# A two-layer attention trunk: PSUM evictions read in steps and written in runs, and the second attention's softmax denominators turned once for four units and applied after the products

## The chip, the cores and the metric

The kernel runs on one core of one Trainium2 chip. The metric is the device time of one execution, in microseconds (us). Before the change three runs gave 1384.46, 1385.28 and 1386.71 us, a median of 1385.28. The profile is one further execution of the same program, which took 1385.48 us; its recorded span is 1383.7 us, and the other 1.8 us lie around it.

Names of engines: PE multiplies matrices (PEld is its weight load), ACT is the scalar engine, DVE the vector engine, POOL the GpSimd engine, and SP issues most DMAs. SBUF is the on-chip memory, PSUM the small memory into which PE writes its products; ACT and DVE evict them from there.

## The reference, cut to what matters

Two layers on a sequence of 1024 tokens of width 1024, everything in float32. Layer 0 is a dilated window attention with 18 heads in three groups of six, layer 1 a latent attention with 16 heads over all 1024 keys.

```python
def dilated_window_attention(q, k, v, bias_table, window, dil):
    ...
    def to_sub(t):
        return t.reshape(B, L, dil, H, Dh).transpose(0, 2, 3, 1, 4)
    ...
def mixer_mla(u, w_in, q_norm, w_uq, kv_norm, w_ukv, w_out):
    ...
        s = (jnp.einsum('bqhd,bkhd->bhqk', qn, k_nope)
             + jnp.einsum('bqhd,bkd->bhqk', qr, k_rope)).astype(jnp.float32) * scale
        p = jax.nn.softmax(s, axis=-1).astype(v.dtype)
        return jnp.einsum('bhqk,bkhd->bqhd', p, v)
    ...
    y = o * jax.nn.silu(gate)
    return y @ w_out
def reference(...):
    for i in range(DEPTH):
        ...
        u = x * (1 + scale) + shift
        ...
        x = layernorm(DEEPNORM_ALPHA * x + gate * y, ln_g[i], ln_b[i])
```

The dilation (4 in the second group, 16 in the third) means that a query meets only the keys of its own class, position modulo the dilation. In layer 1 the softmax divides each query's products by the sum of its 1024 exponentials; the result is multiplied by the gate.

## The kernel before, in words

Every large product is done as three products of float32r halves: a value is split into a high part (ACT casts it) and a low part (DVE or POOL subtracts), and `mm3` (lines 89 to 91) multiplies high by high, high by low and low by high into one PSUM bank.

The order on PE and SP is the order of the program text. ACT, DVE and POOL are ordered at build time by a scheduler that simulates the engines; what it chose is fixed in the built program, and each engine then works strictly in that order. On SP a DMA that waits holds up all DMAs behind it.

**First attention (about 73 to 480 us).** Pairs of heads p = 0 to 8, three pairs to a group. While PE attends for pair p, it also projects q, k and v of pair p+1: each projection is a 128x512 half (`hf`) in a PSUM bank named `pj`, evicted by `a_evac`. For the second group (g = 1, dilation 4) and the third (g = 2, 8 classes) the eviction sorts tokens by class: `a_view` gives the place in SBUF, `src` the order in which the bank is read. Before the change the bank is read in runs and SBUF is written in steps: neighbours in the bank land 256 elements apart (g = 1) or 128 (g = 2). The q of g = 1 goes through ACT twice (line 381, `qh`, one head each, 64x512) and DVE twice (line 383, `ql`), the k likewise (lines 390 and 392), v through ACT once (line 368), and in g = 2 q through ACT (line 371) and k through DVE (line 373). POOL copies `qh` once more (line 386). The same DVE also splits the transposed probabilities of the running attention (line 541, `pt0l`), which PE needs for the products of lines 564 and 572.

Between the two attentions, `merge_lines` combines the three groups' softmax weights. Its line 703 is run three times on 48x128: for g = 0 it reads one operand in a run, for g = 1 and 2 in steps of 32 and 16 elements; it always writes a run.

**Second attention (about 800 to 1290 us).** 128 units u (head u // 8, block u % 8 of 128 queries). `front(u)` is the six score products into a bank pair `s`; `soft(u)` takes the row maximum (DVE, line 1274, `mb`); `expo(u)` takes the exponential of 128x1024 on ACT (line 1280) and leaves the row sums in a column of `mb`; `middle(u-2)` transposes the probabilities (8 PE transposes, line 1293), ACT casts them (line 1296, `pth`) and DVE subtracts (line 1297, `ptl`); `back(w)`, once for two units, does 16 products with v (line 1316) into a bank `o` (named `po` in the code). In `middle` DVE also takes the reciprocal of one unit's row sums (line 1298) and POOL spreads it over 64 columns of `den` (line 1299). `back` transposes `den` on PE (line 1308) ahead of its products, so that the reciprocals lie along the queries; ACT copies both halves of `o` out (lines 1321, 1322, `osum`), DVE multiplies the reciprocals from PSUM with the gate `gT` (line 1325, twice per `back`), and POOL adds the halves and multiplies (lines 1328, 1329). The banks of `t`, `o` and of the projections for coming heads (`m`, made by `b_turn` and `b_qk` in between) come from one ring of four.

`b_weights(p)` fetches the weights of head pair p from DRAM (`wuraw`, `wvraw`, one buffer each) and splits them (ACT; POOL, line 1134, `wul`).

**Tail (about 1290 to 1384 us).** `b_out_blocks(i)` is the output projection of token block i into `po` (two bank pairs in turn, so block i+2 needs block i evicted); its inputs are `ytb`, the split of `gT` (lines 1386, 1387), and the split weights `wo`. `finish(i)` evicts `po` times the gate row (DVE, line 1425, `zb`), adds `x1(i)` (POOL, lines 1419 and 1420, from rows `lnrow` and the DMA `xn_d`), and normalises. SP issues four `lnrow` DMAs (line 801), the gate `row` (line 796) and the `x` blocks (line 1418).

Of the kernel before, what the change touches and what calls it, by code (L numbers as in the profile page):

```python
# [66 lines left out]
class Trunk:  # L67
# [900 lines left out]
    def layer_b_in(self):  # L968
# [3 lines left out]
        nb = self.M.tile([P, 384], F32, name="normb")  # L972
        nc.sync.dma_start(nb, A["bnorm"].to_broadcast([P, 384]))
        nc.vector.tensor_scalar(nb[:, 0:256], nb[:, 0:256], 96.0**-0.5, None, op0=ALU.mult)
        ktab = self.M.tile([P, 8, 2, 16], F32, name="ktab")
# [148 lines left out]

    def b_weights(self, p):

        nc, A, BS = self.nc, self.A, self.BS
        raw = BS.tile([P, 640], F32, tag="wuraw", bufs=1, name=self.nm("wuraw"))
        h = BS.tile([P, 640], F32R, tag="wuh", bufs=1, name=self.nm("wuh"))
        l = BS.tile([P, 640], F32R, tag="wul", bufs=1, name=self.nm("wul"))  # L1130
        n = 384 if p % 2 else 640
        nc.sync.dma_start(raw[:, 0:n], A["wu_o" if p % 2 else "wu_e"][p // 2])
# [3 lines left out]
        if p % 2 == 0:  # L1136
            raw = BS.tile([P, 256], F32, tag="wvraw", bufs=1, name=self.nm("wvraw"))
            h = BS.tile([P, 256], F32R, tag="wvh", bufs=1, name=self.nm("wvh"))
            l = BS.tile([P, 256], F32R, tag="wvl", bufs=1, name=self.nm("wvl"))
            nc.sync.dma_start(raw, A["wv"][p // 2])  # L1140
            nc.scalar.activation(h, raw, AF.Copy)
            nc.gpsimd.tensor_tensor(l, raw, f32(h), op=ALU.subtract)
            self.wv[p // 2] = (h, l)

# [110 lines left out]
    def layer_b_attention(self):  # L1255
        nc = self.nc
        st = {}
# [19 lines left out]
        def expo(u):  # L1277
            s, m = st[u]
            pr = self.ht(F32, "pr")
            nc.scalar.activation(pr, s, AF.Exp, bias=m[:, 0:1], accum_out=m[:, 1:2])  # L1280
            st[u] = (pr, m)

        def middle(u):
            pr, m = st.pop(u)
            a = u % 2
            if a == 0:
                st["pt"] = [(self.gt(F32R, "pth"), self.gt(F32R, "ptl")) for _ in range(2)]
                st["den"] = self.M.tile([P, P], F32, tag="den", bufs=3, name=self.nm("den"))
# [9 lines left out]
            nc.vector.reciprocal(m[:, 2:3], m[:, 1:2])  # L1298
            nc.gpsimd.tensor_copy(st["den"][:, 64 * a : 64 * a + 64], m[:, 2:3].to_broadcast([P, 64]))  # L1299
            if a:  # L1300
                st[("pv", u // 2)] = (st.pop("pt"), st.pop("den"))

        def back(w):
            pts, den = st.pop(("pv", w))
# [3 lines left out]
            nc.tensor.transpose(po[:, 256:384], den, self.ident)  # L1308
            hq = hd % 4
            n = 0  # L1310
            for j in range(2):
                for c in range(4):
                    kt = 4 * j + c
                    v = self.vq[kt // 2][:, (kt % 2) * 512 + hq * P : (kt % 2) * 512 + hq * P + P]
                    for x in range(2):
                        nc.tensor.matmul(po[:, 0:256], v, pts[j][x][:, c * 256 : c * 256 + 256], start=n == 0, stop=n == 15)  # L1316
# [4 lines left out]
            nc.scalar.copy(w3[mine, 0:256], po[other, 0:256])  # L1321
            nc.scalar.copy(w3[mine, 512:768], po[mine, 0:256])
            for a in range(2):
                qs = slice(a * P, a * P + P)
                nc.vector.tensor_tensor(
                    w3[mine, 256 + a * P : 384 + a * P], po[64 * a : 64 * a + 64, 256:384], g[:, qs], op=ALU.mult
                )
            nc.gpsimd.tensor_tensor(w3[mine, 0:256], w3[mine, 512:768], w3[mine, 0:256], op=ALU.add)
            nc.gpsimd.tensor_tensor(g, w3[mine, 0:256], w3[mine, 256:512], op=ALU.mult)
# [4 lines left out]
        for u in range(nu + 4):  # L1334
# [70 lines left out]
    def layer_b_out(self):  # L1405
# [59 lines left out]
        for i in range(7):  # L1465
# [4 lines left out]
            x1(i + 1)  # L1470
            for _ in active:
# [86 lines left out]
```

## Time and profile before

| what | us |
|---|---|
| median of three runs | 1385.28 |
| the profiled execution, total | 1385.48 |
| its span | 1383.7 |
| PE busy | 1340.7 |
| DVE busy | 916.6 |
| ACT busy | 813.4 |
| POOL busy | 578.2 |

How to read the lines below. A row of the waits view says who waited for whom: microseconds in total, how many times, the longest. A row of the timeline is start, duration, engine, line, operation, tiles, shapes, count, and in brackets the idle time before it and what ended it. Matmuls overlap in PE's pipeline, so a matmul's duration is longer than the step from its start to the next start; the steps between starts are what PE's time is made of. A row of the windows view gives for one stretch its length, the busy time of PE, PEld, DVE, ACT and POOL with instruction counts, PE's granted clock (1.00 is full), the DMA share and GB/s. A row of one source line gives its durations in ns (shortest/median/longest), first and last start, and the shapes.

### The profile page before, as it was taken

To read this page: it belongs to the slowest core of one execution; us is meant where nothing else is said; L and a number is where in the kernel's file an instruction comes from. 1 tells how busy PE (TensorE), PEld (TensorE's weight loads), DVE (VectorE), ACT (ScalarE), POOL (GpSimd) and SP (SyncE) were. 2 spreads that over 40 slices of the span, in tenths; PEclk is the share of its full clock that TensorE was granted. 3 is DMA by queue.
4 is the path that set the end of the run, shared out by engine and by line. 5 is a ranking of instruction groups with operands and counts; after the bars stand their busy time and mean duration, and the time that the engine had idled before them with its cause. 6 is when DMAs were issued, how large, how long until landed. Compare 5 with 4: busy or idle time off the path is not lost.

```text
span 1383.7 us, 20921 instructions
## 1 busy us (share of the span) xinstructions
PE 1340.7 (97%) x7439; PEld 1148.6 (83%) x7439; DVE 916.6 (66%) x1688; ACT 813.4 (59%) x1599; POOL 578.2 (42%) x666
## 2 busy tenths in 40 slices
PE   6999999999999999999999999999999999999896
PEld 5788888788888788888988888888889888898785
DVE  6654355455455434666744279888988889888787
ACT  3575566565443432345742288788687878888321
POOL 4442333133122266714732344634553463444653
PEclk9999999999999999999999999999999999999999
DMA  9423221122244255553154011010011000014132
GB/s 354 118 59 49 48 61 40 27 58 77 96 150 125 87 138 141 198 170 118 57 151 145 4 29 22 16 30 17 22 30 31 22 16 17 16 62 145 39 113 86
DMA packets 42168, 110.05 MB, mean 80 GB/s; under 512 B 6277, under 2 KB 12565, under 8 KB 42064
## 3 DMA queue, kind: packets, MB, share of 16 engines
q1 hardware_dynamic: 37512, 96.43, 22.7%
q0 software_dynamic: 4096, 12.24, 3.6%
q8 instruction: 59, 0.97, 0.3%
q14 instruction: 45, 0.37, 0.1%
q10 hardware_dynamic: 456, 0.05, 0.0%
HBM read 92.22 MB, written 8.61 MB: 73 GB/s over the span
## 4 chain that ended last, share of the span: by engine, by line
PE 70%; DVE 15%; ACT 6%; issue 5%; DMA 3%; SPq 0%; DVEq 0%; ACTq 0%
PE pj L89 7%; PE pj L91 7%; PE pj L90 7%; PE o L1316 5%; PE t L1293 5%; DVE mb L1274 3%; PE s L91 3%; PE s L89 3%; PE s L90 3%; PE po L91 3%; PE po L89 3%; PE po L90 3%; PE pg L89 2%; PE pg L91 2%; PE pg L90 2%
## 5 line engine op out<-in xcount | busy, mean ns | idle before, releaser
L89 PE MATMUL pj<-uh,wh 128*128 128x512 f32 x528 | 217.7, 412 | 0.0
L91 PE MATMUL pj<-uh,wl 128*128 128x512 f32 x528 | 207.6, 393 | 0.0
L90 PE MATMUL pj<-ul,wh 128*128 128x512 f32 x528 | 207.3, 393 | 0.0
L1297 DVE TENSOR_TENSOR ptl<-t,pth 128x512 fp32r<-128x512 f32 x256 | 165.3, 681 | 3.0 <-ACT pth L1296 0.9
L1274 DVE TENSOR_REDUCE mb<-s 128x1 f32<-128x1024 f32 x128 | 155.7, 1217 | 7.9 <-PE s L91 6.3
L1280 ACT ACTIVATE pr<-s,mb 128x1024 f32<-128x1024 f32 x128 | 143.4, 1120 | 29.4 <-DVE mb L1274 17.9
L1296 ACT CAST pth<-t 128x512 fp32r<-128x512 f32 x256 | 138.9, 589 | 36.2 <-PE t L1293 34.0
L102 POOL TENSOR_TENSOR wl<-wraw,wh 128x1024 fp32r<-128x1024 f32 x43 | 108.8, 2536 | 91.1 <-ACT wh L101 58.4
L1293 PEld LDWEIGHTS t<-ident,pr 128*128 128x128 f32 x1024 | 119.3, 140 | 19.7 <-DVE ptl L1297 2.6
L1293 PE MATMUL t<-ident,pr 128*128 128x128 f32 x1024 | 133.2, 273 | 1.9 <-DVE ptl L1297 1.9
L1316 PE MATMUL o<-pth,vq 128*128 128x256 f32 x512 | 130.4, 293 | 0.0
L1316 PE MATMUL o<-ptl,vq 128*128 128x256 f32 x512 | 125.5, 283 | 0.8 <-DVE ptl L1297 0.8
L514 ACT ACTIVATE sb<-sb,stat 128x256 f32<-128x256 f32 (+1 forms) x144 | 67.0, 466 | 100.2 <-DVE stat L508 100.1
L91 PEld LDWEIGHTS pj<-uh,wl 128*128 128x128 f32 x528 | 99.4, 188 | 22.3
L1299 POOL COPY den<-mb 128x64 f32<-128x64 f32 x128 | 30.0, 236 | 203.5 <-DVE mb L1298 193.9
L90 PEld LDWEIGHTS pj<-ul,wh 128*128 128x128 f32 x528 | 100.2, 190 | 14.1
L89 PEld LDWEIGHTS pj<-uh,wh 128*128 128x128 f32 x528 | 100.0, 189 | 14.0
L89 PE MATMUL s<-kb,q 128*128 128x512 f32 x256 | 104.5, 408 | 0.4 <-ACT pr L1280 0.4
L91 PE MATMUL s<-kb,q 128*128 128x512 f32 x256 | 101.3, 396 | 0.0
L90 PE MATMUL s<-kb,q 128*128 128x512 f32 x256 | 100.9, 394 | 0.0
L1316 PEld LDWEIGHTS o<-ptl,vq 128*128 128x128 f32 x512 | 97.8, 191 | 1.4 <-DVE ptl L1297 1.4
L1316 PEld LDWEIGHTS o<-pth,vq 128*128 128x128 f32 x512 | 97.7, 191 | 0.2
(286 smaller groups left out, 3252.7 us busy)
## 6 DMA issues: line engine op xcount, KB each, us to landing
wraw<-wa SPq DMA_DIRECT2D x36, 512.0 KB
ada<-ada_row SPq DMA_DIRECT2D x64, 256.0 KB
wraw<-wo_a SPq DMA_DIRECT2D x18, 512.0 KB
ada<-ada_ss SPq DMA_DIRECT2D x16, 512.0 KB
kb<-kb POOLq DMA_DIRECT2D x30, 256.0 KB, 3.0
f<-f_d SPq DMA_DIRECT2D x18, 256.0 KB
xc<-xt SPq DMA_DIRECT2D x8, 512.0 KB
xr<-x SPq DMA_DIRECT2D x8, 512.0 KB
```

The source lines that it names most:

```text
L89: mm(out, wh, xh, start=start, stop=False)
L90: mm(out, wh, xl, start=False, stop=False)
L91: mm(out, wl, xh, start=False, stop=stop)
L102: (lo_engine or self.nc.gpsimd).tensor_tensor(l[:, :width], raw[:, :width], f32(h[:, :width]), op=ALU.subtract)
L514: nc.scalar.activation(sb[:, a * w : a * w + w], sb[:, a * w : a * w + w], AF.Exp, bias=stat[:, 0, hh, t : t + 1], scale=-1.0, accum_out=s ...
L1274: nc.vector.tensor_reduce(m[:, 0:1], s, axis=AX.X, op=ALU.max, negate=True)
L1280: nc.scalar.activation(pr, s, AF.Exp, bias=m[:, 0:1], accum_out=m[:, 1:2])
L1293: nc.tensor.transpose(pt[:, c * P : c * P + P], pr[:, kt * P : kt * P + P], self.ident)
L1296: nc.scalar.copy(h, src)
L1297: nc.vector.tensor_tensor(l, src, f32(h), op=ALU.subtract)
L1299: nc.gpsimd.tensor_copy(st["den"][:, 64 * a : 64 * a + 64], m[:, 2:3].to_broadcast([P, 64]))
L1316: nc.tensor.matmul(po[:, 0:256], v, pts[j][x][:, c * 256 : c * 256 + 256], start=n == 0, stop=n == 15)
```

## The change

Two things are changed together, with some moves beside them.

1. In `a_view` and `a_evac` the loops over class and position are exchanged. The same elements go to the same places; now the bank is read in steps (4 or 8 elements of 4 bytes) and SBUF is written in runs of 128 or 64.
2. In the second attention the exponentials' row sums go to a tile `den` of eight columns for a head. After every fourth unit DVE takes one reciprocal of four columns. `back` no longer transposes for each pair; every second `back` transposes four columns (4x128) behind its products. `spread` copies these four rows to SBUF (ACT), writes them to DRAM and reads them back into 64 partitions (two DMAs on SP, `den_d` and `rden`). POOL multiplies the gate in at once, and five units later `normalise` multiplies 64x512 of the result by `rden`. Line 1325 and the copies of line 1299 are gone. `normalise(31)` is done in the tail.
3. `b_wload` issues a head pair's weight DMAs one pair earlier than before. `normb` and `ktab` share the two `rden` buffers.

```diff
         if g == 1:
-            return t[:, 0:1024].rearrange("p (r j) -> p j r", r=4)[:, hf * 128 : hf * 128 + 128, :]
-        return t[:, 0:1024].rearrange("p (i j) -> p j i", i=8)[:, hf * 64 : hf * 64 + 64, :]
+            return t[:, 0:1024].rearrange("p (r j) -> p r j", r=4)[:, :, hf * 128 : hf * 128 + 128]
+        return t[:, 0:1024].rearrange("p (i j) -> p i j", i=8)[:, :, hf * 64 : hf * 64 + 64]
...
-        src = ps if g == 0 else ps.rearrange("p (j r) -> p j r", r=4 if g == 1 else 8)
+        src = ps if g == 0 else ps.rearrange("p (j r) -> p r j", r=4 if g == 1 else 8)
...
+                self.wuraw = {}
+                self.b_wload(0)
                 self.b_weights(0)
...
+    def b_wload(self, p):
+        if p >= NPAIR_B:
+            return
...
+        raw = BS.tile([P, 640], F32, tag="wuraw", bufs=1, name=self.nm("wuraw"))
+        n = 384 if p % 2 else 640
+        self.nc.sync.dma_start(raw[:, 0:n], A["wu_o" if p % 2 else "wu_e"][p // 2])
...
     def b_weights(self, p):
...
+        raw, rv, n = self.wuraw.pop(p)
...
+        self.b_wload(p + 1)
...
     def layer_b_attention(self):
         nc = self.nc
-        st = {}
+        st, dens, rden = {}, {}, {}
+        den_d = self.DR.tile([32, 512], F32, name="den_d")
...
         def expo(u):
             s, m = st[u]
+            if u % 8 == 0:
+                dens[u // 8] = self.M.tile([P, 8], F32, tag="den", bufs=3, name=self.nm("den"))
             pr = self.ht(F32, "pr")
-            nc.scalar.activation(pr, s, AF.Exp, bias=m[:, 0:1], accum_out=m[:, 1:2])
-            st[u] = (pr, m)
+            nc.scalar.activation(pr, s, AF.Exp, bias=m[:, 0:1], accum_out=dens[u // 8][:, u % 8 : u % 8 + 1])
+            st[u] = pr
+            if u % 4 == 3:
+                d = dens[u // 8][:, u % 8 - 3 : u % 8 + 1]
+                nc.vector.reciprocal(d, d)
+
+        def spread(v, bank):
+            hd = v // 2
+            t = rden[v] = self.M.tile([P, 512], F32, tag="rden", bufs=2, name=self.nm("rden"))
+            mine, other = slice(64 * (hd % 2), 64 * (hd % 2) + 64), 64 - 64 * (hd % 2)
+            rows = t[other : other + 4, 0:P]
+            nc.scalar.copy(rows, bank[0:4, 256:384])
+            nc.sync.dma_start(den_d[v].rearrange("(a b) -> a b", b=P), rows)
+            nc.sync.dma_start(t[mine, :], den_d[v : v + 1, :].to_broadcast([64, 512]))
+
+        def normalise(v):
+            hd = v // 2
+            mine = slice(64 * (hd % 2), 64 * (hd % 2) + 64)
+            g = self.gT[hd // 2][mine, v % 2 * 512 : v % 2 * 512 + 512]
+            nc.gpsimd.tensor_tensor(g, g, rden.pop(v)[mine, :], op=ALU.mult)
...
-            nc.vector.reciprocal(m[:, 2:3], m[:, 1:2])
-            nc.gpsimd.tensor_copy(st["den"][:, 64 * a : 64 * a + 64], m[:, 2:3].to_broadcast([P, 64]))
...
         def back(w):
...
-            nc.tensor.transpose(po[:, 256:384], den, self.ident)
...
+            if w % 2:
+                nc.tensor.transpose(po[0:4, 256:384], dens[hd][:, 2 * (w % 4) - 2 : 2 * (w % 4) + 2], self.ident)
             mine, other = slice(64 * e, 64 * e + 64), slice(64 - 64 * e, 128 - 64 * e)
+            if w % 2:
+                spread(w // 2, po)
...
-            for a in range(2):
-                qs = slice(a * P, a * P + P)
-                nc.vector.tensor_tensor(
-                    w3[mine, 256 + a * P : 384 + a * P], po[64 * a : 64 * a + 64, 256:384], g[:, qs], op=ALU.mult
-                )
...
+            nc.gpsimd.tensor_tensor(g, w3[mine, 0:256], g, op=ALU.mult)
...
+            if u >= 11 and u % 4 == 3:
+                normalise((u - 11) // 4)
...
+        self.b_last = lambda: normalise(31)
```

Three places show how the instructions stand now. The numbers behind names are the build's buffer numbers.

PE, early in the second attention, around one `back`. Before, the transpose of `den` stands between the transposes of the probabilities (`t`) and the products with v (`o<-pth,vq`):

```order
L1293 MATMUL t_6851<-ident,pr_6808 128x128 x4
L1293 MATMUL t_6858<-ident,pr_6808 128x128 x4
L1308 MATMUL o_6869<-ident,den_6791 128x128
L1316 MATMUL o_6869<-pth_6787,vq_6717 128x256
L1316 MATMUL o_6869<-ptl_6788,vq_6717 128x256
```

Now, at every second `back`, it stands behind the products and ahead of the next unit's scores (`s`):

```order
L1349 MATMUL o_6944<-pth_6850,vq_6723 128x256
L1349 MATMUL o_6944<-ptl_6851,vq_6723 128x256
L1352 MATMUL o_6944<-ident,den_6733 4x128
L89 MATMUL s_6971<-kb_5393,q_6626 128x512
L90 MATMUL s_6971<-kb_5394,q_6626 128x512
```

Sixty-four transposes became 32, and nothing else moved on PE in the whole program.

DVE, while `b_qk` prepares the next heads: `kb` is the split of a projection that frees its bank for PE. Before:

```order
L1298 RECIPROCAL mb_7195<-mb_7195 128x1
L1274 TENSOR_REDUCE mb_7234<-s_7221 128x1
L1245 TENSOR_TENSOR kb_6149<-m_7217,kb_6148 64x512
L1245 TENSOR_TENSOR kb_5394<-m_7217,kb_5393 64x512
L1297 TENSOR_TENSOR ptl_7237<-t_7241,pth_7236 128x4x128
L1298 RECIPROCAL mb_7234<-mb_7234 128x1
L1297 TENSOR_TENSOR ptl_7239<-t_7248,pth_7238 128x4x128
L1274 TENSOR_REDUCE mb_7291<-s_7284 128x1
L1325 TENSOR_TENSOR osum_7277<-o_7259,gT_6076 64x128 x2
```

Now:

```order
L1289 TENSOR_REDUCE mb_7112<-s_7099 128x1
L1259 TENSOR_TENSOR kb_6149<-m_7095,kb_6148 64x512
L1259 TENSOR_TENSOR kb_5394<-m_7095,kb_5393 64x512
L1333 TENSOR_TENSOR ptl_7115<-t_7118,pth_7114 128x4x128
L1333 TENSOR_TENSOR ptl_7117<-t_7125,pth_7116 128x4x128
```

The single reciprocals and line 1325 have left the stream; one reciprocal of four columns stands in it for every four units.

SP, at the end of the second attention. Before, the tail's loads follow the last weights:

```order
L1376 DMA woraw_12718<-wo_b 128x1024
L1376 DMA woraw_12720<-wo_b 128x1024
L801 DMA lnrow_12905<-ln 128x1024
L801 DMA lnrow_12907<-ln 128x1024
L801 DMA lnrow_12909<-ln 128x1024
L801 DMA lnrow_12911<-ln 128x1024
L796 DMA row_12913<-rows_d 128x1024
```

Now the last two spreads stand ahead of them; the second waits for the last `back`:

```order
L1311 DMA den_d<-rden_12433 4x128
L1312 DMA rden_12433<-den_d 64x512
L1412 DMA woraw_12451<-wo_b 128x1024
L1412 DMA woraw_12453<-wo_b 128x1024
L1311 DMA den_d<-rden_12595 4x128
L1312 DMA rden_12595<-den_d 64x512
L801 DMA lnrow_12633<-ln 128x1024
L801 DMA lnrow_12635<-ln 128x1024
L801 DMA lnrow_12637<-ln 128x1024
L801 DMA lnrow_12639<-ln 128x1024
L796 DMA row_12641<-rows_d 128x1024
```

The four `lnrow` loads and the gate `row` moved behind the last `back` and its round trip through DRAM.

More of the change, by code (lines that the diff above doesn't have):

```diff
@@ L1135, in b_weights @@
         self.wu[p] = (h, l)
-        if p % 2 == 0:
-            raw = BS.tile([P, 256], F32, tag="wvraw", bufs=1, name=self.nm("wvraw"))
+        if rv is not None:
             h = BS.tile([P, 256], F32R, tag="wvh", bufs=1, name=self.nm("wvh"))
             l = BS.tile([P, 256], F32R, tag="wvl", bufs=1, name=self.nm("wvl"))
-            nc.sync.dma_start(raw, A["wv"][p // 2])
-            nc.scalar.activation(h, raw, AF.Copy)
-            nc.gpsimd.tensor_tensor(l, raw, f32(h), op=ALU.subtract)
+            nc.scalar.activation(h, rv, AF.Copy)
+            nc.gpsimd.tensor_tensor(l, rv, f32(h), op=ALU.subtract)
             self.wv[p // 2] = (h, l)
+        self.b_wload(p + 1)
     def b_v(self, quad):
@@ L1297, in middle @@
                 nc.vector.tensor_tensor(l, src, f32(h), op=ALU.subtract)
-            nc.vector.reciprocal(m[:, 2:3], m[:, 1:2])
-            nc.gpsimd.tensor_copy(st["den"][:, 64 * a : 64 * a + 64], m[:, 2:3].to_broadcast([P, 64]))
             if a:
-                st[("pv", u // 2)] = (st.pop("pt"), st.pop("den"))
+                st[("pv", u // 2)] = st.pop("pt")
         def back(w):
-            pts, den = st.pop(("pv", w))
+            pts = st.pop(("pv", w))
             hd, t0 = w // 4, (w % 4) * 256
@@ L1321, in back @@
             nc.scalar.copy(w3[mine, 0:256], po[other, 0:256])
[L1322 to L1329 removed]
+            nc.scalar.copy(w3[mine, 256:512], po[mine, 0:256])
+            nc.gpsimd.tensor_tensor(w3[mine, 0:256], w3[mine, 256:512], w3[mine, 0:256], op=ALU.add)
+            nc.gpsimd.tensor_tensor(g, w3[mine, 0:256], g, op=ALU.mult)
         nu = 128
@@ L1470, in layer_b_out @@
             x1(i + 1)
+            if i == 0:
+                self.b_last()
             for _ in active:
```

19 lines of the change are left out of this document (11 added, 8 removed).

## The prediction

> **What bounds the kernel now.** First the page's busy times, then stretches, then PE's waits.
>
> ```profile
> PE 1340.7 (97%) x7439; PEld 1148.6 (83%) x7439; DVE 916.6 (66%) x1688; ACT 813.4 (59%) x1599; POOL 578.2 (42%) x666
> ```
>
> ```profile
> core 0: us, PE busy (x) PEld busy (x) DVE busy (x) ACT busy (x) POOL busy (x), PEclk, DMA share, GB/s
> ...
> 73.00:230.00 157.00, 153.69 (x854) 130.59 (x853) 74.66 (x188) 93.77 (x207) 49.00 (x68) 1.00 0.21 43
> ...
> 800.00:1285.00 485.00, 479.25 (x3153) 426.03 (x3153) 425.67 (x738) 397.51 (x761) 223.62 (x347) 1.00 0.13 36
> ```
>
> PE is the bound nearly everywhere: in the second attention it is busy for 479.25 of 485 us at full clock. DVE, with 425.67, is close behind. So a microsecond is gained in two ways only: PE work that goes, or a PE wait that goes. The waits are few:
>
> ```profile
> PE o L572 <- DVE pt0l L541: 3.8, 4, 1.1
> ...
> PE po L89 <- DVE zb L1425: 3.0, 1, 3.0
> PE m L89 <- DVE kb L1245: 2.5, 7, 0.4
> ...
> PE t L1293 <- DVE ptl L1297: 1.9, 3, 0.6
> PE o L564 <- DVE pt0l L541: 1.2, 1, 1.2
> ...
> PE o L1316 <- DVE ptl L1297: 0.8, 3, 0.3
> ```
>
> Two groups bear on the change: 5.0 us (3.8 + 1.2) in the first attention, 5.2 (2.5 + 1.9 + 0.8) in the second, and 3.0 once in the tail. Each wait is a little longer than its row says, since a matmul's duration overlaps the next one's start.
>
> **Evictions by class.** One of the five first-attention waits in full:
>
> ```profile
> 218.25 2.20 ACT L381 ACTIVATE qh<-pj 64x512 fp32r<-64x512 f32 x2 [0.87 <-PE pj L91]
> ```
>
> ```profile
> 220.48 2.15 DVE L383 SCALAR_TENSOR_TENSOR ql<-pj,qh 64x512 fp32r<-64x512 f32 x2 [2.38 <-PE s L501]
> 222.66 0.69 DVE L541 TENSOR_TENSOR pt0l<-t,pt0h 128x512 fp32r<-128x512 f32 x1
> ```
>
> ```profile
> 222.04 0.36 PE L572 MATMUL o<-pt0h,vt 128*128 128x256 f32 x1
> 223.41 0.39 PE L572 MATMUL o<-pt0l,vt 128*128 128x256 f32 x1 [1.01 <-DVE pt0l L541]
> ```
>
> PE's product waits for `pt0l`, which stands on DVE behind two stepped evictions of together 2.15 us, which began when ACT's two (2.20 us) were done. From start to start PE took 1.37 us; the step without a wait is 0.12 (below), so 1.25 are lost. The other four show the same picture (two stepped `ql` or `k` on DVE, then `pt0l`). What an eviction costs in steps and in runs stands in one row each, since the first group evicts the same 64x512 in runs:
>
> ```profile
> L381 ACT ACTIVATE qh<-pj x20: 575/1073/1093, 74.9 to 276.1; 64x512 fp32r<-64x512 f32 x20
> L383 DVE SCALAR_TENSOR_TENSOR ql<-pj,qh x20: 681/1054/1099, 76.2 to 278.3; 64x512 fp32r<-64x512 f32 x20
> ```
>
> In runs ACT takes 0.58 and DVE 0.68, written in steps 1.07 and 1.05. If reading PSUM in steps costs nothing, DVE's pair falls by 0.75 and ACT's by 1.0; `pt0l` comes up to 1.75 us earlier, more than the 1.25 lost, and all five waits go: 5.0 by the rows, 5 x 1.25 = 6.2 at most; I take **-5.5**. No row shows a stepped read of PSUM. The nearest is a stepped read of SBUF:
>
> ```profile
> L703 DVE TENSOR_TENSOR Y<-Y,X x3: 282/364/384, 491.0 to 491.5; 48x128 f32<-48x128 f32 x3
> ```
>
> Shortest is the read in a run, the other two read in steps: +0.09 for 128 elements, so +0.37 for 512, which is what a stepped write costs (1.05 - 0.68). By that row the edit only moves the price from the write to the read, and gains 0. Between these ends I take the first, because the stepped operand now lies in another memory, and keep the other as the first rival. [...] The casts on ACT and POOL that also get shorter are not waited for.
>
> **Denominators.** What a transpose of `den` costs PE is read from starts:
>
> ```profile
> 1047.29 1.03 PE L1293 MATMUL t<-ident,pr 128*128 128x128 f32 x8
> 1048.16 0.27 PE L1308 MATMUL o<-ident,den 128*128 128x128 f32 x1
> ...
> 1048.39 0.28 PE L1316 MATMUL o<-ptl,vq 128*128 128x256 f32 x1
> ```
>
> Between 1047.29 and 1048.39 lie nine transposes and one product; products follow each other at 0.12, so a transpose costs (1.10 - 0.12) / 9 = 0.11. Of 64, 32 go; the 32 that stay turn four columns against the same 128 of `ident`, and I count them the same. 32 x 0.11 = **-3.5**. Bounds: 0 if a 4-column one costs double, -7 if it costs nothing.
>
> DVE loses two groups and gains 32 reciprocals:
>
> ```profile
> L1325 DVE TENSOR_TENSOR osum<-o,gT 64x128 f32<-64x128 f32 x128 | 36.8, 287 | 35.7 <-ACT osum L1322 32.2 <-POOL den L1299 1.2
> ...
> L1298 DVE RECIPROCAL mb<-mb 128x1 f32<-128x1 f32 x128 | 20.0, 156 | 6.5 <-ACT pr L1280 3.7
> ```
>
> 36.8 + 20.0 - 32 x 0.16 = 51.7 us less, 374 of 485, and it no longer idles for ACT's `osum` in front of L1325. That touches PE's second group of waits. One of the seven `m` waits:
>
> ```profile
> 836.39 1.39 DVE L1245 TENSOR_TENSOR kb<-m,kb 64x512 fp32r<-64x512 f32 x2
> ```
>
> ```profile
> 837.29 0.28 PE L1316 MATMUL o<-ptl,vq 128*128 128x256 f32 x1
> 837.93 0.47 PE L89 MATMUL m<-lath,wuh 128*128 128x512 f32 x1 [0.36 <-DVE kb L1245]
> ```
>
> DVE ends at 837.78 what should have ended before 837.41; it needs 0.4 us, and L1298 and L1325 ahead of it take more. Of the 5.2 us I take **-4**; bounds 0 and -7 (the hidden parts with it).
>
> What is added. ACT: 32 copies of 4x128 ahead of `osum`, priced by its 128x128 cast:
>
> ```profile
> L1045 ACT CAST lath<-plt 128x128 fp32r<-128x128 f32 x24 | 6.4, 267 | 7.6 <-DVE latl L1046 7.6
> ```
>
> 32 x 0.27 = 8.6 us, so ACT has 406 of 485. The copy waits for the late transpose; behind it in ACT's order stand `osum` and the next `pth`, for which DVE and then PE wait. ACT's 79 idle us hide it; if they never did, it would cost the whole 8.6. The bank of `o` is free once ACT has copied, without DVE. I take **+1**. POOL: 32 normalises of 64x512 against the copies of line 1299:
>
> ```profile
> L1226 POOL TENSOR_TENSOR q<-ab,q 64x512 fp32r<-64x512 f32 x16 | 20.3, 1290 | 1.3 <-ACT q L1224 0.9
> ```
>
> 32 x 1.29 = 41 us on an engine with 224 of 485; behind a normalise that waits for its DMA stand only `osum` sums, and it comes five units after its spread. SP holds each read until its write has landed; behind it stand weights that are fetched a pair ahead.
>
> `b_wload` makes SP hold the second `wuraw` until POOL has split the first, and `qtab`, the next `wgraw` and the ada loads stand behind it:
>
> ```profile
> 733.55 1.57 POOL L1134 TENSOR_TENSOR wul<-wuraw,wuh 128x640 fp32r<-128x640 f32 x1 [14.74 <-ACT wuh L1133]
> ```
>
> ```profile
> 742.95 1.05 ACT L1118 ACTIVATE wgh<-wgraw 128x1024 fp32r<-128x1024 f32 x1
> ```
>
> From 735.1 to 742.95 are 7.8 us for a load that takes about 4 (tail): 0, and at worst nothing PE sees before its next gate block.
>
> **The tail.** SP now waits for the last `back` before it fetches the rows of the tail:
>
> ```profile
> 1269.95 4.31 SPq L801 DMA_DIRECT2D lnrow<-ln  x4
> ...
> 1323.32 0.32 SPq L1418 DMA_DIRECT2D x<-xn_d  x1
> ```
>
> ```profile
> 1291.49 0.36 ACT L1321 COPY osum<-o 64x256 f32<-64x256 f32 x1
> ```
>
> ```profile
> f_d<-Y POOLq DMA_DIRECT2D x3, 24.0 KB, 1.7
> ```
>
> ```profile
> 1327.36 2.67 POOL L1419 TENSOR_TENSOR x<-x,lnrow 128x1024 f32<-128x1024 f32 x1 [13.76 <-DMA x<-xn_d]
> ```
>
> ```profile
> 1305.78 1.22 DVE L1425 TENSOR_TENSOR zb<-po,row 128x1024 f32<-128x1024 f32 x1
> ```
>
> In the old positions: the copy at 1291.49 + 0.27, the write lands 1.7 later at 1293.5, then the loads go out 24 us later than today. A load of 512 KB takes 4.0 us (1323.32 to 1327.36); if those behind follow 1.5 us apart (an estimate from the 354 GB/s of the page's first slice) the first row is there at 1297.7 and the gate row, the fifth, at 1303.7. `zb(0)`, for which PE waits its 3.0 us, starts at 1305.78 today. ACT scales the first two rows between its `ytb` casts, and DVE has one more `ytb` ahead of `zb(0)`, so it starts between 1304 and 1309: -2 to +3; since POOL's sums, beside which DVE's `ytb` take over 2 us, also start later, I take **-1**.
>
> ```profile
> GB/s 354 118 59 49 48 61 40 27 58 77 96 150 125 87 138 141 198 170 118 57 151 145 4 29 22 16 30 17 22 30 31 22 16 17 16 62 145 39 113 86
> ```
>
> **Sum**: -5.5 - 3.5 - 4 + 1 - 1 = -13, against the profiled execution's 1385.48: **1372.5 us** (the median of the runs lies 0.2 lower, which I leave out).
>
> **The rivals.** *Stepped reads cost what stepped writes cost.* [...] -13 + 5.5 = -7.5: 1378.0. *The copy on ACT is not hidden* and the first rival holds too: 1378.0 + 7.6 (8.6 for the 1 counted) = 1385.6; no difference. For it: ACT's order is strict, and the copy stands ahead of `pth`. Against it: 79 idle us. It is also where the change would end if it freed DVE and nobody waited for DVE. *Stepped reads cost more, and the kernel gets slower.* There are 12 halves of q and k in g = 1, each with two evictions on ACT and two on DVE in a row ahead of `pt0l`; if each took d more than today, PE would wait about 3d more per half, 36d in all. The other terms sum to -7.5; the point is d = 0.21, a read of 1.26 us, and from 1.34 it shows. At three steps of price in place of today's two (0.68, 1.05, so 1.42) d is 0.37: +13.3 - 7.5 = 1391. Nothing speaks for it but that no row shows such a read.
>
> **How the numbers follow.** Forecast 0.52 (its own range 1367 to 1377), the first rival 0.26, no difference 0.13, slower 0.09. A measurement of this kernel can tell about 0.2%, 2.8 us. Faster 0.78, same 0.13, slower 0.09. The range takes the forecast and the first rival whole, with the bounds of waits and of the tail: 1367 to 1383, which leaves out the last two cases.
>
> **What would show it.** Lines 381 and 383 with medians at 0.58 and 0.68, and no wait of lines 564 and 572 for `pt0l`: the first term; medians at 1.05 or above: the rivals. PE's steps around the 4-column transpose: 0.11 each. No `m` wait for `kb`; DVE near 374 us in the stage. In the tail PE's wait for `zb`, and the row DMAs issued behind the last read of `den_d`. I am wrong if PE waits for ACT's `pth` in the second attention, or for a row in the tail.

## The result, and the profile after

The changed kernel took 1375.09 us (median of four runs, 1373.93 to 1375.52), the kernel before, run beside it, 1384.95 (1384.46 to 1386.71). The ratio is 0.9928 with a 95% interval of 0.9913 to 0.9944: 9.9 us less, where 13 had been forecast. The profiled execution took 1375.37 us, with a span of 1373.3.

The page's busy times of the changed kernel, and the windows row of its second attention:

```profile
PE 1329.1 (97%) x7407; PEld 1138.4 (83%) x7407; DVE 863.1 (63%) x1464; ACT 799.6 (58%) x1631; POOL 584.4 (43%) x570
```

```profile
800.00:1285.00 485.00, 477.75 (x3124) 422.82 (x3122) 381.67 (x519) 401.44 (x790) 238.02 (x252) 1.00 0.15 37
```

DVE lost 44 us in that window (425.67 before; 51.7 were forecast), POOL gained 14. PE's waits in the changed kernel, the rows that answer to those of before:

```profile
PE m L89 <- DVE kb L1259: 3.0, 7, 0.5
...
PE t L1329 <- DVE ptl L1333: 1.9, 3, 0.6
PE po L89 <- DVE zb L1461: 1.9, 2, 1.2
PE o L1349 <- DVE ptl L1333: 1.1, 2, 0.8
```

The rows of lines 564 and 572 (5.0 us) are gone. The three of the second attention are still there, and larger (6.0 after 5.2).

Where the time went is read from five stages. PE's order bounds them: the first and the last high-by-high `pj` product, the first `s`, the last product with v, the end. The source view of before and of after gives their starts in its last two numbers of a row.

```profile
L89 PE MATMUL pj<-uh,wh x528: 387/395/742, 68.7 to 556.1; 128*128 128x512 f32 x176
...
L89 PE MATMUL s<-kb,q x256: 390/393/503, 800.1 to 1272.8; 128*128 128x512 f32 x128
...
L1316 PE MATMUL o<-pth,vq x512: 278/283/366, 813.3 to 1290.9; 128*128 128x256 f32 x171
```

```profile
L89 PE MATMUL pj<-uh,wh x528: 387/395/486, 67.5 to 547.8; 128*128 128x512 f32 x176
...
L89 PE MATMUL s<-kb,q x256: 392/397/501, 791.9 to 1260.6; 128*128 128x512 f32 x128
...
L1349 PE MATMUL o<-pth,vq x512: 274/283/387, 804.6 to 1278.5; 128*128 128x256 f32 x171
```

| stage | before | after | difference |
|---|---|---|---|
| to the first `pj` | 68.7 | 67.5 | -1.2 |
| first attention (first to last `pj`) | 487.4 | 480.3 | -7.1 |
| to the first `s` | 244.0 | 244.1 | +0.1 |
| second attention (first `s` to last product) | 490.8 | 486.6 | -4.2 |
| tail, to the end of the span | 92.8 | 94.8 | +2.0 |

They add up to -10.4, the difference of the spans (1383.7 and 1373.3).

### The profile page after: what moved, and what is told of

Its sections match the earlier page's. It is cut to its first block, busy times and chain, and to the rows that moved or that the text cites. A ratio compares the mean times of both kernels' runs of the same rounds, so it can differ in the third digit from the quotient of the medians.

```text
span 1373.3 us, 20420 instructions
## 1 busy us (share of the span) xinstructions
PE 1329.1 (97%) x7407; PEld 1138.4 (83%) x7407; DVE 863.1 (63%) x1464; ACT 799.6 (58%) x1631; POOL 584.4 (43%) x570
## 4 chain that ended last, share of the span: by engine, by line
PE 74%; DVE 11%; ACT 7%; DMA 4%; issue 3%; SPq 0%; DVEq 0%; ACTq 0%
PE pj L89 8%; PE pj L91 8%; PE pj L90 8%; PE o L1349 6%; PE t L1329 5%; PE s L89 3%; PE s L91 3%; PE s L90 3%; PE po L91 3%; PE po L90 3%; PE po L89 3%; PE pg L89 2%; PE pg L91 2%; PE pg L90 2%; DMA ada<-ada_row 2%
## 5 line engine op out<-in xcount | busy, mean ns | idle before, releaser
L1360 POOL TENSOR_TENSOR osum<-osum 64x256 f32<-64x256 f32 x64 | 47.7, 745 | 168.6 <-ACT osum L1359 167.6
```

The costliest lines, as they stand in the source:

```text
L1360: nc.gpsimd.tensor_tensor(w3[mine, 0:256], w3[mine, 256:512], w3[mine, 0:256], op=ALU.add)
```

## The experiments

Twelve more runs followed, each with the kernel before run beside it on the same chip; its medians there were 1383.98 to 1384.21 us. Their profiles cut into the same stages:

| run | median us | to first `pj` | first att. | to first `s` | second att. | tail |
|---|---|---|---|---|---|---|
| before | 1384.95 | 68.7 | 487.4 | 244.0 | 490.8 | 92.8 |
| after | 1375.09 | 67.5 | 480.3 | 244.1 | 486.6 | 94.8 |
| after_again | 1374.33 | 67.3 | 478.2 | 244.0 | 487.1 | 95.3 |
| evict_only | 1376.82 | 66.9 | 479.6 | 243.6 | 491.0 | 93.9 |
| den_only | 1382.65 | 67.7 | 485.2 | 244.0 | 486.4 | 95.2 |
| no_turn | 1373.59 | 69.5 | 479.6 | 244.0 | 484.2 | 94.8 |
| dve_load | 1391.33 | 68.2 | 479.8 | 244.1 | 503.4 | 95.1 |
| dve_half | 1377.06 | 68.1 | 479.1 | 244.0 | 489.7 | 95.5 |
| copy_dve | 1374.15 | 67.3 | 479.0 | 244.0 | 485.9 | 94.1 |
| kb_first | 1395.88 | 67.3 | 479.7 | 244.0 | 507.4 | 95.0 |
| m_later | 1383.58 | 69.0 | 482.9 | 244.0 | 494.9 | 95.3 |
| kb_pair | 1373.12 | 67.7 | 478.3 | 244.1 | 484.3 | 95.2 |
| tail_rows | 1374.53 | 69.2 | 481.4 | 244.0 | 486.4 | 94.1 |
| probe (one execution) | - | 67.1 | 481.2 | 244.0 | 486.2 | - |

**How far a stage repeats.** after_again is the changed kernel once more. No run touches the startup, and it takes 66.9 to 69.5 us: a single profile can be off by 2 us there. The second attention of the runs that leave it as the change has it (after, after_again, den_only, tail_rows, probe) takes 486.2 to 487.1, mean 486.5; in its old form it takes 490.8 (before) and 491.0 (evict_only). So a difference of less than about 0.7 us says nothing in that stage, and one of less than 2 says nothing in a total from one profile.

> The changed kernel once more, for the others of this group to be compared with, and to see how far its stages repeat. Both theories: 1374 to 1376 us. Startup (to the first pj product) 67 to 69 us, first attention 399 to 401, second attention 486.5 from its first scores to its last product, the rest 94 to 95.

The 399 to 401 us of that text count the first attention to an earlier end than the table's last `pj`; the second attention came out 0.6 us and the tail 0.3 us longer than expected.

### The two halves of the change alone

evict_only is the kernel before with the three lines of `a_view` and `a_evac`; den_only is the changed kernel with those three lines taken back.

```diff
-            return t[:, 0:1024].rearrange("p (r j) -> p j r", r=4)[:, hf * 128 : hf * 128 + 128, :]
+            return t[:, 0:1024].rearrange("p (r j) -> p r j", r=4)[:, :, hf * 128 : hf * 128 + 128]
...
-        src = ps if g == 0 else ps.rearrange("p (j r) -> p j r", r=4 if g == 1 else 8)
+        src = ps if g == 0 else ps.rearrange("p (j r) -> p r j", r=4 if g == 1 else 8)
```

> Before with the evictions by classes alone. Theory A (the five first-attention waits for pt0l went because stepped PSUM reads cost what reads in runs cost): lines 371 to 392 at 0.58 to 0.69 us, no wait of lines 564 and 572 for pt0l, the first attention 6 to 7 us shorter, 1378 to 1379 us in all. Rival B (part of the first attention's gain comes from the later stages' other order): under 5 us, above 1380.

> After with the old evictions, so the denominators' part alone. Theory A (32 transposes at 0.11 us go, 3.5 us; the second attention's waits stay; the tail loses about 2): 1385 - 3.5 - 0.6 + 2 = 1383, 1382 to 1384. Rival B (the waits are gained as predicted and the tail gains too, and the rest of the difference is chance): 1377 to 1379.

evict_only: ratio 0.9948 (0.9933 to 0.9964), 7.2 us less; its 1376.82 us is a little under its theory's 1378 to 1379. den_only: 0.9984 (0.9975 to 0.9994), 1.3 us less at the medians; it is inside its theory's range. PE's waits in the first attention (67 to 480 us), first of evict_only, whole, then of den_only, whole:

```profile
PE t L525 <- ACT sb L514: 4.3, 3, 1.7
PE o L553 <- DVE pt L528: 0.3, 1, 0.3
```

```profile
PE o L572 <- DVE pt0l L541: 3.8, 4, 1.0
PE t L525 <- ACT sb L514: 3.1, 3, 1.3
PE o L564 <- DVE pt0l L541: 1.2, 1, 1.2
PE o L553 <- DVE pt L528: 0.7, 1, 0.7
```

The five waits for `pt0l` go with the evictions and stay without them. What an eviction costs now, from the source view of the changed kernel:

```profile
L381 ACT ACTIVATE qh<-pj x20: 572/593/599, 73.7 to 269.1; 64x512 fp32r<-64x512 f32 x20
L383 DVE SCALAR_TENSOR_TENSOR ql<-pj,qh x20: 681/688/695, 75.0 to 270.4; 64x512 fp32r<-64x512 f32 x20
```

Shortest (in runs, first group), median and longest lie within 0.03 us of each other: reading the bank in steps of 4 elements took 0.02 us more on ACT than in runs and 0.01 on DVE, where writing SBUF in steps had taken 0.50 and 0.37 more.

### What a read in steps costs

probe is the changed kernel with a piece behind its end (its output has no part in it):

```diff
...
+        for r in (1, 2, 4, 8, 16, 32):
+            for src in (ps, sb[:, 0:512]):
+                x = src.rearrange("p (j r) -> p r j", r=r) if r > 1 else src
+                y = o[:, 0:512].rearrange("p (r j) -> p r j", r=r) if r > 1 else o[:, 0:512]
+                nc.scalar.copy(y, x)
+                nc.vector.tensor_copy(y, x)
+                nc.vector.tensor_tensor(y, x, y, op=ALU.subtract)
```

> After, with a piece of its own behind the end: 128x512 copied in runs from PSUM and from SBUF by ACT, by DVE, and through a DVE subtraction, read in steps of 1, 2, 4, 8, 16 and 32 elements; results unused. Theory A (a read of PSUM costs the same at every step, one of SBUF pays from 4 elements on): PSUM within 0.05 us of 0.58 on ACT and 0.69 on DVE at every step; SBUF 0.35 to 0.5 more from 4 on. Rival B (reads pay nowhere, only writes do): SBUF as PSUM. Rival C (PSUM pays at larger steps): more at 16 and 32.

The source view, `qp` the bank in PSUM, `qs` the tile in SBUF, six steps each:

```profile
L1526 ACT COPY qo<-qp x6: 585/585/586, 1369.3 to 1392.8; 128x512 f32<-128x512 f32 x6
L1526 ACT COPY qo<-qs x6: 618/1054/1107, 1372.3 to 1394.9; 128x512 f32<-128x512 f32 x6
```

```profile
L1528 DVE TENSOR_TENSOR qo<-qp,qo x6: 691/691/692, 1371.6 to 1394.1; 128x512 f32<-128x512 f32 x6
L1528 DVE TENSOR_TENSOR qo<-qs,qo x6: 691/1020/1074, 1373.4 to 1396.6; 128x512 f32<-128x512 f32 x6
```

From PSUM 0.585 on ACT and 0.691 on DVE at every step from 1 to 32 elements. From SBUF ACT takes 0.62, 0.65, 1.09, 1.11, 1.05 and 1.06 in that order, so the price comes in between 2 and 4 elements and does not grow. DVE's subtraction takes 0.69 up to 2 elements and 1.02 to 1.07 from 4 on, its plain copy (line 1527) 0.43 and then 0.59 to 0.62; from PSUM that copy takes 0.68 to 0.69 at every step. Theory A, but with less of a price for SBUF on DVE: 0.33 to 0.38 us in the subtraction, 0.16 to 0.19 in the copy. Only steps inside one bank were tried.

### The transposes

```diff
-            if w % 2:
-                nc.tensor.transpose(po[0:4, 256:384], dens[hd][:, 2 * (w % 4) - 2 : 2 * (w % 4) + 2], self.ident)
...
-            nc.scalar.copy(rows, bank[0:4, 256:384])
+            nc.scalar.copy(rows, bank[0:4, 0:128])
```

> After without the 32 transposes of the denominators (rden is copied from the products, so the output is not the reference's). Theory A (a 4-column transpose costs PE 0.105 us, 0.025 to the next start and 0.08 more in the step behind that, as much as a 128-column one): 32 x 0.105 = 3.4 us less in the second attention, 483 us. Rival B (it costs only the 0.025 of its own step): 0.8 less, 485.7; Rival C (the m waits swallow what goes): between.

The second attention took 484.2, that is 2.3 less than 486.5: Rival C. The timeline of the changed kernel shows what one of them costs where nothing waits:

```profile
812.99 0.27 PE L1352 MATMUL o<-ident,den 128*4 128x128 f32 x1
813.01 0.48 PE L89 MATMUL s<-kb,q 128*128 128x512 f32 x1
813.33 0.39 PE L90 MATMUL s<-kb,q 128*128 128x512 f32 x1
```

The next matmul starts 0.02 us behind the transpose, but the step after that is 0.32 where 0.23 follow otherwise. Together 0.105 (0.025 and 0.08), the same as the 0.11 of a 128-column one, though most of it falls in the step behind. Seven of the 32 stand in front of the `m` waits, where a microsecond saved is waited (the seven waits grew from 3.0 to 3.8 us in no_turn); 25 x 0.105 = 2.6, and 2.3 were measured.

### What DVE's relief was worth

copy_dve moves line 1310's copy from ACT to DVE. dve_load and dve_half add a product of `ptl` with `ident`, 64x128, to DVE behind line 1333, two and one per unit (the second diff is dve_half's; in dve_load the two lines stand inside the loop over the halves).

```diff
-            nc.scalar.copy(rows, bank[0:4, 256:384])
+            nc.vector.tensor_copy(rows, bank[0:4, 256:384])
```

```diff
                 nc.vector.tensor_tensor(l, src, f32(h), op=ALU.subtract)
+            z = self.M.tile([64, P], F32, tag="zz", bufs=2, name=self.nm("zz"))
+            nc.vector.tensor_tensor(z, f32(l)[0:64, 0, :], self.ident[0:64, :], op=ALU.mult)
```

> After, with the 32 copies rden of the turned denominators on DVE instead of ACT. Two accounts of the second attention, where 4.2 us went and 3.7 of them are the transposes: Theory A (the relief of DVE was worth nothing, and the copies on ACT cost nothing either): 486 to 487.5 us from the first scores to the last product, 1374 to 1375 in all. Rival B (DVE's relief was worth the 3 to 4 us of the prediction, and the copies, which stand ahead of osum and pth on ACT, took them back): 483 to 484, about 1371.

> After, with two more 64x128 products on DVE per unit in the second attention (256 in all, some 50 us, about what line 1325 and the reciprocals took), results unused. Theory A (PE's waits there are set by order and latency, and DVE's load is beside the point): second attention within 1 us of 486.5, 1374 to 1376. Rival B (the prediction's own: DVE's load makes the waits, so freeing it had to gain 4 us, and something else took them): the second attention 3 to 5 us longer, 1378 to 1380.

> After, with one 64x128 product more on DVE per unit in the second attention (128 in all, some 38 us by the 0.3 us that the run with 256 showed, so that DVE has about 420 us of 485, as before the change), results unused. Theory A (up to the load of before, PE's waits don't hang on DVE's load, and the 17 us of the run with 256 come from a DVE that is full): 486 to 489 us, 1374 to 1377. Rival B (each microsecond on DVE costs PE the same share, 17 of 76): 495 us, 1383.

copy_dve: 485.9, 0.6 less, which is within chance; the copies on ACT took back next to nothing, close to its Theory A. dve_load: 503.4, 16.9 more, which neither side expected. Its windows row, and that of dve_half:

```profile
800.00:1285.00 485.00, 469.38 (x3039) 411.30 (x3038) 457.91 (x763) 395.13 (x776) 235.18 (x246) 1.00 0.13 35
```

```profile
800.00:1285.00 485.00, 476.68 (x3117) 421.47 (x3117) 423.99 (x644) 401.06 (x788) 236.54 (x250) 1.00 0.14 36
```

In dve_half DVE's load is that of before (423.99 and 425.67 us), and the stage took 489.7, 3.2 more: just above Theory A's 489, far under B's 495. The window holds only 485 of dve_load's 503 us, so the loads are better compared over the whole stage, from the first `s` to the last product: 427.9 us before, 382.6 after, 428.0 in dve_half and 468.2 in dve_load. The price of load rises steeply: 3.2 us for the first 45 us of it, 13.7 for the next 40 (with a part of PE's clock in it: the longest `s` product of dve_load took 0.77 us, that of the changed kernel 0.50). So load on DVE is not beside the point, as Theory A had it; yet taking 45 us away brought only some 0.5 (the stage's 4.2 less the 3.7 of the transposes), which is within chance.

The waits say where load is paid for. The seven `m` waits hardly answer to it: 3.0 us in the changed kernel, 3.3 in dve_half, 1.7 in dve_load. The waits for `ptl` do: 3.0, 4.9 and 11.5 us. And the time that DVE gained became idle time: ahead of the row maximum it waits 46 us for the scores in the changed kernel, where it waited 6 before. The added instructions stand right behind `ptl`, ahead of the row maximum, those that the change removed stood elsewhere, and with the load the scheduler also ordered ACT's casts anew at some places. Which of these makes the difference between adding and taking away stays open.

### Why the seven `m` waits stayed

The same place as in the prediction, in the changed kernel: ACT, DVE, PE.

```profile
824.77 0.58 ACT L1257 CAST kb<-m 64x512 fp32r<-64x512 f32 x1
825.37 1.12 ACT L1297 ACTIVATE pr<-s,mb 128x1024 f32<-128x1024 f32 x1
...
826.61 0.58 ACT L1257 CAST kb<-m 64x512 fp32r<-64x512 f32 x1
```

```profile
825.81 1.22 DVE L1289 TENSOR_REDUCE mb<-s 128x1 f32<-128x1024 f32 x1
827.22 1.39 DVE L1259 TENSOR_TENSOR kb<-m,kb 64x512 fp32r<-64x512 f32 x2 [0.19 <-ACT kb L1257]
```

```profile
828.06 0.27 PE L1352 MATMUL o<-ident,den 128*4 128x128 f32 x1
828.75 0.47 PE L89 MATMUL m<-lath,wuh 128*128 128x512 f32 x1 [0.42 <-DVE kb L1259]
```

DVE is idle ahead of `kb`: it waits for ACT, which now takes an exponential between its two casts of `kb`, and it does the row maximum first. Nothing of line 1325 or the reciprocals stands here. In the kernel before there was little of them either: at this place one reciprocal of 0.15 us stood ahead of `kb`, and line 1325 ran 5.6 us earlier, behind an idle time of DVE:

```profile
830.74 0.59 DVE L1325 TENSOR_TENSOR osum<-o,gT 64x128 f32<-64x128 f32 x2 [1.78 <-ACT osum L1322]
```

Three kernels change this place. kb_first pins the row maximum behind both halves' `kb` on DVE; m_later puts PE's next `m` product behind the next scores; kb_pair pins the row maximum of the first half alone and puts the exponential behind both casts on ACT.

```diff
+            self.pin = True
             rope(hf, 1)
...
+            i = nc.vector.tensor_reduce(m[:, 0:1], s, axis=AX.X, op=ALU.max, negate=True)
+            if self.pin:
+                self.tc.keep_in_program_order(i)
```

```diff
             rope(hf, 1)
             yield 0.0
+            if hf == 0:
+                yield 0.0
```

```diff
...
+            if u < 112 and u % 16 == 9:
+                self.tc.keep_in_program_order(i)
...
-                soft(u)
+                soft(u, p + 1 < NPAIR_B and r == 10)
+                if p + 1 < NPAIR_B and r == 10:
+                    expo(u - 1)
...
-            if u < nu:
+            if u < nu and not (p + 1 < NPAIR_B and r == 9):
                 expo(u)
```

> After, with DVE's two kb subtractions put ahead of the row maximum that stands in front of them. Theory A (PE's seven m waits are set by DVE's order behind the end of the scores, 1.2 us of row maximum ahead of kb, not by DVE's load): the m waits for kb go, 7 x 0.7 = 4 to 5 us less in the second attention, 1370 to 1371. Rival B (the row maximum is then late for pr and PE waits for the transposes instead): 1374 to 1377, with new waits of PE for pr or ptl.

> After, with one half's q product of the coming heads put behind the next unit's scores on PE, so that its bank has 2.8 us more to come free. Theory A (the seven m waits are set by when kb is through on ACT and DVE: ACT takes an exponential between its two casts, DVE a row maximum ahead of them; 0.68 us from the turn to the m product where 0.02 is the step without a wait): the seven waits go, 7 x 0.6 = 4 us less in the second attention, 482 to 483 us, 1371 in all. Rival B (PE is late there by as much at the next link, the transposes that wait for pr or ptl): 486, 1375.

> After, with ACT's two kb casts of the first half in a row (the exponential of the unit before is put behind them) and DVE's two kb subtractions ahead of the row maximum. Theory A (at those seven places nothing but this order makes PE wait for the bank): the seven m waits go, 482 to 483 us in the second attention, 1370 to 1371. Rival B (the exponential and the row maximum have no slack either, so a wait for pr or ptl takes their place within two units): 486 us or more, 1374 to 1385.

kb_first lost 20.9 us in the stage and m_later 8.4, both far more than their Rivals B allowed for. Their waits, one row of each:

```profile
PE o L1353 <- DVE kb L1259: 13.5, 7, 2.1
```

```profile
PE t L1331 <- DVE ptl L1335: 11.1, 10, 1.3
```

In kb_first the `m` wait also stayed (3.0, seven times), since ACT's second cast was still behind the exponential. In the second half, where ACT splits a weight first, DVE could no longer put the row maximum ahead of `kb`: it stood idle for 1.3 us until ACT's cast of `kb` was done (835.33), and PE's products with v waited 2.1 us (836.87). Some 7 of the 20.9 us are PE's clock, which fell behind four of these waits (an estimate: four times the 1.7 us worked out for one of them in the last section). In m_later the wait moved on to the transposes and grew. kb_pair shows what the order is worth if both engines keep it:

```profile
826.28 0.27 PE L1356 MATMUL o<-ident,den 128*4 128x128 f32 x1
826.30 0.47 PE L89 MATMUL m<-lath,wuh 128*128 128x512 f32 x1
```

The seven waits are gone and no row of its waits names `kb`; the stage took 484.3, 2.2 less, half of what the seven had cost (7 x 0.67 = 4.7), and between the two expectations. About 0.4 us of each came back at the next `back`, which PE reaches 1.2 us after the start of the transposes ahead of it where 0.8 is the step without a wait. Its median of 1373.12 (1371.38 to 1374.65; ratio 0.9916, 0.9902 to 0.9930) is the lowest of all, but its interval overlaps that of the changed kernel; only the stage shows the gain clear of chance.

### The tail

```diff
-            nc.sync.dma_start(den_d[v].rearrange("(a b) -> a b", b=P), rows)
-            nc.sync.dma_start(t[mine, :], den_d[v : v + 1, :].to_broadcast([64, 512]))
+            def move():
+                nc.sync.dma_start(den_d[v].rearrange("(a b) -> a b", b=P), rows)
+                nc.sync.dma_start(t[mine, :], den_d[v : v + 1, :].to_broadcast([64, 512]))
+
+            if v == 31:
+                self.b_move = move
+            else:
+                move()
...
         gate = self.ada_row(1)
+        self.b_move()
```

> After with the last spread's two DMAs issued behind the four lnrow loads and the gate row instead of ahead of them. Theory A (ACT waits 3.36 us for lnrow with two ytb casts behind it, so DVE reaches the third block late): the third zb eviction moves up by 2 to 4 us against the last product of the second attention, 1371 to 1373 us. Rival B (the tail is set by DVE and POOL work that is there in either order, or PE): no change, 1375.

SP's loads in the changed kernel, and what ACT did meanwhile:

```profile
1279.33 0.27 SPq L1311 DMA_DIRECT2D den_d<-rden  x1
1280.54 0.45 SPq L1312 DMA_DIRECT2D rden<-den_d  x1
1281.09 1.96 SPq L801 DMA_DIRECT2D lnrow<-ln  x4
```

```profile
1286.09 1.06 ACT L1449 ACTIVATE lnrow<-lnrow 128x1024 f32<-128x1024 f32 x1 [3.36 <-DMA lnrow<-ln]
```

The loads went out 2.6 us behind the last product, where before they stood 21.0 ahead of it (1269.95, 1290.9): 23.6 us later, the prediction's 24. ACT waited 3.4 us for the first row with `ytb` casts behind it. `zb(0)` started at 1291.54, 13.0 us behind the last product where it had been 14.9, and PE's wait for it fell from 3.0 to 1.2. The end did not follow. Third `zb` eviction (block 2) of before, after and tail_rows:

```profile
1323.84 1.22 DVE L1425 TENSOR_TENSOR zb<-po,row 128x1024 f32<-128x1024 f32 x1
```

```profile
1313.39 1.22 DVE L1461 TENSOR_TENSOR zb<-po,row 128x1024 f32<-128x1024 f32 x1
```

```profile
1314.23 1.22 DVE L1468 TENSOR_TENSOR zb<-po,row 128x1024 f32<-128x1024 f32 x1
```

From here to the end of the span it is 59.9 us before and 59.9 after, and 60.9 in tail_rows. In this stretch DVE waits some 6 us for ACT and never for PE, before and after: it works through blocks 2 to 7 at its own pace. So the tail is as long as DVE's way to block 2. From the last product that way is 32.9 us before and 34.9 after. In tail_rows it is 33.2, so the order of SP explains 1.7 of the 2.0; that is less than Theory A's 2 to 4. Of the gain 1.0 went again behind block 2, and the whole (1374.53) is Rival B's and cannot be told from the changed kernel. PE's wait for `zb` in tail_rows was 4.5 us, and the end did not feel it.

How far this repeats is seen in the other runs. evict_only, whose tail is the kernel before's, takes 33.0 us to block 2 and 60.9 from there, so the 1.0 behind block 2 also comes without the change; the ten profiles with the changed tail take 34.0 to 35.3 and 59.8 to 60.2. The longer way to block 2 is clear of chance.

By which link the order of SP makes it longer is not shown. ACT's 3.4 us reached DVE as little: 1.05 us idle ahead of the next `ytb`, where 0.70 is usual. From `zb(0)` to `zb(2)` DVE then took 21.9 us where before it took 18.1, and there POOL's sums, which had waited for their `x`, ran beside its work; the sum of block 0 took 3.41 us, where before, with POOL idle, it took 1.22.

```profile
1287.70 0.69 DVE L1423 TENSOR_TENSOR ytb<-gT,ytb 128x512 fp32r<-128x512 f32 x1 [1.05 <-ACT ytb L1422]
```

```profile
1292.88 5.20 POOL L1455 TENSOR_TENSOR x<-x,lnrow 128x1024 f32<-128x1024 f32 x2 [6.78 <-DMA x<-xn_d]
```

```profile
1304.18 3.41 DVE L1462 SCALAR_TENSOR_TENSOR zb<-x,zb 128x1024 f32<-128x1024 f32 x1
```

## Why the prediction held, and where not

- **Evictions, -5.5.** Right, and for its reason: all five waits went. den_only against the changed kernel's kind gives 485.2 - 479.3 = 5.9 (479.3 is the mean of the nine runs with the new evictions in which PE's clock stayed full at the end of that stage, see the last section; den_only's stayed full too). The five steps of before, measured one by one, lose 1.33, 1.25, 0.87, 1.25 and 1.23 us, together 5.9. The profile's -7.1 has about 1.7 of chance in it. The end of the range at 0, which row 703 supported, was wrong: that row is a read of SBUF, and reads of PSUM in steps took what reads in runs take (0.585 us on ACT and 0.691 on DVE at every step of probe).
- **Transposes, -3.5.** Right, by sums over starts: 64 x 0.11 before, 32 x 0.105 now, 3.7 less. Only the 32 that stay were taken out in a run of their own.
- **PE's waits in the second attention, -4.** Wrong; this is the step that failed: "of the 5.2 us I take -4", because DVE loses line 1325 and the reciprocals. The stage's -4.2 less 3.7 leaves 0.5 for everything else, the +1 for ACT's copies included (0.6 by copy_dve). The reading of the `m` wait took line 1325 and the reciprocals for what made `kb` late; just ahead of `kb` stood one reciprocal of 0.15 us, and line 1325 ran 5.6 us earlier. In the changed kernel the wait is set by a chain that does not get shorter with DVE's load: end of the scores, row maximum, and ACT's casts. There the scheduler put an exponential between these casts; with both engines' order mended (kb_pair) the waits went, and half their price came back one link later.
- **The tail, -1.** Wrong, +2.0. The loads were timed well: `zb(0)`, which waited 0.3 us for the gate row, came 1.8 us earlier against the last product, inside the -2 to +3 of the working, and PE's wait fell. But the step "`zb(0)`, for which PE waits" took PE for the bound of the tail. DVE is, and its way to block 2 grew by 2.0 us, 1.7 of them by the order of SP (tail_rows); the link stays open.
- **Startup**: -1.2, chance: no run touches it, and it spreads over 2.6 us.

So 1375.09 against 1372.5: the two mechanical terms held, and the two that turned on who waits for whom were off by 2.5 and 3. Without the two pieces of chance (1.2 and 1.7) the stages of the profiles add up to -7.5 instead of -10.4, just outside the measured interval (-12.0 to -7.8). The runs do not say how much of this chance is also in the medians, so part of the nearness to -13 may be luck.

## What to carry to other kernels

Put the step of a reordering eviction on the PSUM side and write SBUF in runs; here that turned 1.07 us into 0.59 on ACT and 1.05 into 0.69 on DVE. Before pricing a wait by the load of the engine it names, look whether that engine was busy up to the wait and what its last predecessor waited for: here 45 us taken off DVE gained its stage about half a microsecond, and where a wait was removed by force the next link took half of it or more. In a tail, find the engine whose spacing to the end does not change, and price the change by when that engine gets to its first fixed point.

## What the runs showed of the hardware beside that

**PE's clock fell after some short waits, not after each.** The windows view of kb_first around one of its waits of 2.1 us (the ninth number is PE's granted clock):

```profile
836.80:838.00 1.20, 1.13 (x9) 1.17 (x10) 1.18 (x1) 0.08 (x1) 0.00 (x0) 0.93 0.00 0
838.00:840.00 2.00, 2.00 (x10) 1.97 (x10) 1.96 (x3) 1.28 (x3) 0.00 (x0) 0.50 0.00 0
840.00:842.00 2.00, 2.00 (x9) 1.54 (x8) 0.05 (x2) 0.66 (x2) 1.11 (x2) 0.69 0.00 0
```

PE resumes at 836.87 at full speed, is at half from about 838 to 841.2, and then full again: one wait cost 2.1 us and some 1.7 more. Four of kb_first's seven waits there brought such a stretch (2.1, 1.9, 1.9 and 1.9 us long), three did not (2.1, 2.1 and 1.5). The kernel before has one, after a wait of 1.3 us at the end of its first attention:

```profile
472.00:475.00 3.00, 2.94 (x8) 2.29 (x9) 0.42 (x1) 2.48 (x4) 0.00 (x0) 0.59 0.00 0
475.00:478.00 3.00, 3.00 (x16) 2.64 (x16) 0.00 (x0) 1.19 (x1) 0.00 (x0) 0.85 0.00 0
```

(0.41 + 0.15) x 3.0 = 1.7 us, which the changed kernel's profile did not have at that place: that is the chance in the -7.1. Of the fourteen profiles four show it there (before, tail_rows, m_later and probe; the wait was 1.3 us in before and 1.7 in tail_rows), ten run through at 1.00, evict_only with a wait of 1.7. At the clock of 0.50 a 128x512 product of before took 0.63 us, at 1.00 0.39. None of m_later's seven waits of 1.3 us in the second attention brought a fall: its longest `s` product took 0.50 us there, as in before. Nor did before's 3.0 us wait for `zb`, behind which the clock stood at 1.00.

**DVE beside POOL.** A `ytb` of 128x512 took 0.69 us on DVE while POOL was idle and 1.6 to 2.1 while POOL's `x` sums ran (two rows of before; the sums ended at 1313.60):

```profile
1312.04 2.11 DVE L1387 TENSOR_TENSOR ytb<-gT,ytb 128x512 fp32r<-128x512 f32 x1 [0.70 <-ACT ytb L1386]
1314.84 0.69 DVE L1387 TENSOR_TENSOR ytb<-gT,ytb 128x512 fp32r<-128x512 f32 x1 [0.70 <-ACT ytb L1386]
```
